# Gated scan in a hybrid encoder: narrow TensorE products regrouped, key scales moved to the first queries, last columns scaled wider apart

## The chip, the cores and the metric

The kernel runs on one core of a Trainium2 chip. Its time is device time in microseconds (us), the median of several runs. TensorE (PE) multiplies matrices, and its weight loads are shown apart (PEld). VectorE (DVE), ScalarE (ACT) and GpSimd (POOL) work elementwise; SyncE (SP) issues most transfers. Each engine takes its own instructions in their order and waits on semaphores for the others.

## The reference

One encoder layer on x of 1024 positions by 1024 channels, float32:

```
h  = RMSNorm(x);  P = h @ W_in
A  = conv module on its columns (GLU, depthwise conv of 31, LayerNorm, swish, pointwise)
B  = bidirectional gated scan, 8 heads of 128:  S_t = diag(f_t) S_{t-1} + k_t v_t^T,  o_t = S_t^T q_t
     f = lb + (1-lb) sigmoid(z),  k = (1-lb) sigmoid(-z), one scan forward and one backward
x  = x + W_out(sigmoid(gA) * A + sigmoid(gB) * B)
x  = x + W_down(silu(dwconv3(h2 W_gate)) * (h2 W_up)),  h2 = RMSNorm(x);  final RMSNorm
```

## The kernel before

Large products are done in three parts (high times high, high times low, low times high, `mm3`, lines 149 to 151), each a matmul of 128x512. They are the dense work, and the order on TensorE is the order in which the code is written, while the tile framework's scheduler orders the other engines.

The scan is worked off while dense products are still left. A head has 1024 positions, in two halves of 512, so there are 16 halves `i`. For each half two things run side by side:

- `scan_base` prepares keys `kG` (two directions) and queries `qF`: it doubles the span over which gates are multiplied in, 1, 2, 4, 8, 16, in place. Before each doubling ScalarE copies (`woven`, line 1176) the pairs of that level to pages `A` (8 of them in turn). Five steps, each ended by a `yield`. Step 3 issues the score products of the levels up to 4 (`level`, line 1195: 64 products of 32x32, 128 in the trace, where each float32 product shows twice).
- `scan_levels` goes on with the finished half: products of levels 8 and 16 into a bank `ob`, then zeros (`none`, line 1302) and blocks of 32 into a bank `sc`, doubling 32, blocks of 64 (line 1281), doubling 64. `scan_states` then transposes `kG` (line 1320, called kT here) and makes the states from it (line 1329, into `u`).

So a half has five places `n` = 0 to 4, and at the end of each `between` is called: it issues some dense products (`FILL` is 1.77 pieces, a piece is 6 matmuls, so 6 or 12), one step of the next half's preparation (`ahead`), and one step of the outputs of the head before (`pending`: 11 products of line 1370, at places 1 and 2 of even halves, or four transposes of line 1396, at places 1 and 2 of odd halves). The blocks, the levels up to 4 and the first `u` take the two banks `sc` in turn.

At the very end, `last_jobs` makes the last part of the down projection: 8 column jobs for positions 0 to 511, 8 for the next 256, 8 for the last 256 (`PARTS`). A job has 4 pieces. Each job's result is transposed some pieces later (`turn_out`, line 1890), squared on ScalarE (line 1892) and multiplied by the norm weight on VectorE (line 1905). When a part is done, `scale_out` scales each 128 positions by the row's norm, 640 columns on VectorE (line 1928) and 384 on ScalarE (line 1926), and stores them. `later(n, ...)` puts something off by n pieces.

Of the kernel before, what the change touches and what calls it, by code (L numbers as in the profile page):

```python
# [15 lines left out]
ALU = mybir.AluOpType  # L16
# [3 lines left out]
FILL = 1.77  # L20
# [7 lines left out]
GLU_FILL = 2  # L28
GLU_MORE = 4
GLU_LATE = 17  # L30
BASE_STEPS = 1
ALIGN = 128
H = 512
EPS = 1e-6
# [14 lines left out]
def tile_hybrid_encoder(  # L49
# [51 lines left out]
    def bank(tag):  # L101
        return ps.tile([P, H], F32, tag=tag, name=nm(tag), bufs=BANKS[tag])
# [56 lines left out]
    def later(n, do):  # L159

        chores.append([n, do])
# [981 lines left out]
    def tt(o, a, b, op=ALU.mult):  # L1143
        V.tensor_tensor(o, a, b, op=op)  # L1144
# [7 lines left out]
    def scan_inputs(i):  # L1152


        h, half = divmod(i, 2)
        q = page(hp, "q", 2)
        f = hp.tile([P, 2, H], F32, tag="f", name=nm("f"), bufs=2)
        kG = hp.tile([P, 2, H], F32, tag="kG", name=nm("kG"), bufs=3)
        nc.sync.dma_start(q, d_q[h][half])
        for d in range(2):  # L1160
            z = page(hp, "zi", 3)
            nc.sync.dma_start(z, d_z[d][h][half])
            A.activation(kG[:, d, :], z, AF.Sigmoid, scale=-1.0)
            A.activation(z, z, AF.Sigmoid)
            A.activation(f[:, d, :], z, AF.Identity, scale=oml_of(d, h), bias=lb_of(d, h))
        V.tensor_scalar(f, f, MIN_FORGET, 1.0, op0=ALU.max, op1=ALU.min)
        return q, f, kG, kscale[:, h : h + NH + 1 : NH]

    def pairs(t, h, other=H):

        return view(t, 0, [[other + h, 2], [2 * h, H // (2 * h)], [1, h]])
# [7 lines left out]
    def slot(b, n):  # L1179
        return b[:, n * P : (n + 1) * P]  # L1180
# [7 lines left out]
    def each():  # L1188
        for c in range(4):
            for g in range(0, P, 32):  # L1190
                yield c * P + g, slice(g, g + 32), slice(32 * c, 32 * c + 32)

    def level(b, A_t, Q_t):
        for at, g, o in each():
            T.matmul(b[g, o], A_t[:, at : at + 32], Q_t(at), start=True, stop=True)

    def row(t):
        return lambda at: t[:, at : at + 32]
# [18 lines left out]
    def scan_base(ins):  # L1217


        q, f, kG, ks = ins  # L1220
        qF = hp.tile([P, 2, H], F32, tag="qF", name=nm("qF"), bufs=4)
        D_t = hp.tile([P, 4, 32], F32, tag="D", name=nm("D"), bufs=3)
        for d in range(2):
            V.tensor_scalar(kG[:, d, :], kG[:, d, :], ks[:, d : d + 1], None, op0=ALU.mult)
        k_d, Q1 = page(hp, "A", 8), page(hp, "A", 8)
        tt(k_d, kG[:, 0, :], kG[:, 1, :], ALU.add)
        A1 = woven(kG, 1)
        odd = H // 2
        tt(
            pairs(Q1, 1, 0),  # L1230
            view(q, 0, [[1, 2], [2, odd], [1, 1]]),
            view(f, H, [[1 - H, 2], [2, odd], [1, 1]]),
        )
        tt(
            view(qF, 1, [[H - 1, 2], [2, odd]]),
            view(q, 1, [[-1, 2], [2, odd]]),
            view(f, H + 1, [[-(H + 1), 2], [2, odd]]),
        )
# [24 lines left out]
        A16, Q16 = woven(kG, 16), woven(qF, 16)  # L1263
        yield
        double_keys(kG, tb, 16)
        double_queries(qF, pairs(qF, 16), tb, 16)
        tb = totals(tb, 16)
        yield qF, kG, tb, D_t, A8, Q8, A16, Q16

    def scan_levels(base, S_t, Tt):  # L1270


        qF, kG, tb, D_t, A8, Q8, A16, Q16 = base

        def blocks(b, h):

            for c in range(0, H, P):
                for s0 in range(0, P, h):
                    t0 = s0 ^ h
                    d = s0 // h % 2  # L1280
                    T.matmul(  # L1281
                        b[s0 : s0 + h, c + t0 : c + t0 + h],
                        kG[:, d, c + s0 : c + s0 + h],
                        qF[:, 1 - d, c + t0 : c + t0 + h],
                        start=True,
                        stop=True,
                    )

        def double(tb, h, to=None):
            double_keys(kG, tb, h)  # L1290
            double_queries(qF, pairs(qF, h), tb, h)
            return totals(tb, h, to)

        b = bank("ob")
        level(slot(b, 0), A8, row(Q8))
        level(slot(b, 1), A16, row(Q16))
        for n, m in enumerate((m_8, m_16)):
            V.copy_predicated(D_t, over(m), near(slot(b, n)))
        yield
        b = bank("sc")  # L1300
        for at, g, _ in each():
            T.matmul(b[g, at : at + 32], none, none, start=True, stop=True)
        blocks(b, 32)
        tb = double(tb, 32)
        yield
        blocks(b, 64)
        double(tb, 64, view(Tt, 0, [[4, 2], [1, 4]]))
        A.copy(S_t, c4(b))
        for g in range(0, P, 32):
            nc.scalar.dma_start(S_t[g : g + 32, :, g : g + 32], D_t[g : g + 32])  # L1310
        yield
# [126 lines left out]

    NI = 2 * NH
    cur = Base(scan_inputs(0))  # L1440
    ins = scan_inputs(1)
    dense.fill(7)
    for pieces in (3, 4, 4, 3, 0):
        cur.step(1)
        dense.fill(pieces)
    pending = Stream(iter(()))
    for h in range(NH):
        Tt = hp.tile([P, 2, 2, 4], F32, tag="Tt", name=nm("Tt"), bufs=4)
        Sf = [hp.tile([P, 4, DK], F32, tag="st", name=nm("Sf"), bufs=4) for _ in range(2)]
        Sb = [hp.tile([P, 4, DK], F32, tag="st", name=nm("Sb"), bufs=4) for _ in range(2)]  # L1450
        kept = []
        for half in range(2):
            i = 2 * h + half
            base = cur.result()
            ahead = Base(ins) if i + 1 < NI else None
            ins = scan_inputs(i + 2) if i + 2 < NI else None

            def between(fill):
                dense.fill(fill)
                if ahead is not None:  # L1460
                    ahead.step(BASE_STEPS)
                pending.fill(1)

            S_t = hp.tile([P, 4, P], F32, tag="S", name=nm("S"), bufs=3)
            vl = load(d_v[h][half])
            for n, _ in enumerate(scan_levels(base, S_t, Tt[:, half])):
                if n == 1:
                    b = bank("tr")
                    for c in range(4):
                        T.transpose(b[:, c * P : (c + 1) * P], vl[:, c * P : (c + 1) * P], ident)  # L1470
                    v = hp.tile([P, 4, DK], F32, tag="v", name=nm("v"), bufs=3)
                    A.copy(v.rearrange("p c e -> p (c e)"), b)
                between(FILL)
            qF, kG = base[:2]
            for _ in scan_states(i, kG, v, Tt, Sf, Sb):
                between(FILL)
            kept.append((S_t, v, qF))
            cur = ahead
        pending = Stream(outputs(h, kept, Tt, Sf, Sb))

    dense.owed = 0
# [395 lines left out]
    def final_evac(i, half, chunks, acc):  # L1877
        t = xr[i][half][:, chunks[0] * P : (chunks[-1] + 1) * P]
        V.tensor_tensor(t, acc, t, op=ALU.add)
        later(4, lambda: turn_out(i, half, chunks))  # L1880

    def turn_out(i, half, chunks):

# [114 lines left out]
    fy = tc.alloc_tile_pool(name="fy", bufs=1, reuse_waits="tile")  # L1998
    st = Stream(run_jobs(last_jobs(LAST0, final_evac)))
    for n, part in enumerate(PARTS[:-1]):  # L2000
        st.fill(4 * ND * (n + 1) + 3 - st.count)
        finish(*part, late=2 + 2 * n)
    st.drain()
    advance_chores(1 << 10)
    finish(*PARTS[-1], late=0)
# [34 lines left out]
```

## Time and profile before

| | |
|---|---|
| median of 3 runs | 1736.81 us (1735.74 to 1737.69) |
| profiled execution | 1736.41 us, its span 1734.3 us |
| TensorE busy | 1709.2 us, 99% of the span; granted clock 0.998 |
| VectorE, ScalarE, GpSimd busy | 1255.9, 830.3, 170.4 us |
| scan, 505 to 860 us: TensorE, VectorE, ScalarE busy | 352.59, 286.16, 248.60 of 355 us |

TensorE is hardly ever idle, so a row of the timeline is best read by its start: the step from one start to the next is what an instruction costs in the stream (0.23 us for a dense matmul of 128x512, though its own row says 0.39).

### The profile page before, as it was taken

The page shows a single profiled execution, that of the slowest core. Times are in us where ns is not written, and L with a number is a line of the kernel's source. Part 1 is how long each engine was busy: PE and PEld are TensorE (multiplying, and loading weights), DVE is VectorE, ACT ScalarE, POOL GpSimd, SP SyncE. Part 2 cuts the span into 40 slices and gives each one's busy share as a digit, 9 for nine tenths or more (in the row PEclk, how much of TensorE's full clock was granted, in tenths as well). Part 3 has the DMA queues.
Part 4 walks back from the last instruction along what each step waited for, and adds up shares of the span by engine and source line. Part 5 has one row for each costly group of instructions (what it writes and reads, how often), then busy time and mean ns, then how long its engine had stood idle before and what let it go on. Part 6 is the DMA issues. An engine that isn't in the chain of part 4 may idle for free.

```text
span 1734.3 us, 30669 instructions
## 1 busy us (share of the span) xinstructions
PE 1709.2 (99%) x11902; PEld 1415.0 (82%) x11902; DVE 1255.9 (72%) x1937; ACT 830.3 (48%) x1544; POOL 170.4 (10%) x185
## 2 busy tenths in 40 slices
PE   8999999999999999999999999999999999999997
PEld 6878888888788888888878888888888888888787
DVE  5599999746778888888557466667767776657865
ACT  7444443334566777776442245444434433542334
POOL 2211111100000000000000002011111111000110
PEclk9999999999999999999999999999999999999999
DMA  8768888854673444435579466568777776783842
GB/s 288 239 167 184 193 194 193 197 167 154 207 230 104 131 126 132 127 115 192 175 248 333 147 207 205 146 148 170 158 170 160 180 172 153 229 267 107 205 91 98
DMA packets 343751, 308.27 MB, mean 178 GB/s; under 512 B 25262, under 2 KB 255798, under 8 KB 343606
## 3 DMA queue, kind: packets, MB, share of 16 engines
q1 hardware_dynamic: 289590, 267.51, 48.7%
q0 software_dynamic: 44800, 37.76, 15.2%
q10 hardware_dynamic: 9216, 1.05, 0.4%
q8 instruction: 93, 1.52, 0.4%
q14 instruction: 52, 0.43, 0.1%
HBM read 201.40 MB, written 87.03 MB: 166 GB/s over the span
## 4 chain that ended last, share of the span: by engine, by line
PE 44%; DMA 2%; DVE 2%; ACT 1%; issue 1%; SPq 0%; POOL 0%; POOLq 0%; ACTq 0%; DVEq 0%
PE mm L151 10%; PE mm L150 10%; PE mm L149 10%; PE sc L149 3%; PE sc L150 3%; PE sc L151 3%; PE tr L149 1%; PE tr L150 1%; PE tr L151 1%; DMA tm<-d_bm 1%; DVE hx L125 0%; DMA wr<-in_ffn_w_down_dram 0%; DMA wr<-wr 0%; DMA d_gc<-ft 0%; DVE wp L125 0%
## 5 line engine op out<-in xcount | busy, mean ns | idle before, releaser
L149 PE MATMUL mm<-hx,wp 128*128 128x512 f32 x1068 | 428.0, 401 | 3.3 <-ACT tm L851 2.1
L151 PE MATMUL mm<-hx,wp 128*128 128x512 f32 x1068 | 418.1, 391 | 0.9 <-DVE wp L125 0.8
L150 PE MATMUL mm<-hx,wp 128*128 128x512 f32 x1068 | 416.9, 390 | 0.3 <-DVE hx L125 0.2
L125 ACT CAST wp<-wr 128x1024 fp32r<-128x1024 f32 (+2 forms) x147 | 147.2, 1002 | 259.2 <-PE mm L150 119.5
L151 PEld LDWEIGHTS mm<-hx,wp 128*128 128x128 f32 x1068 | 200.9, 188 | 46.3 <-DVE wp L125 3.4
L149 PEld LDWEIGHTS mm<-hx,wp 128*128 128x128 f32 x1068 | 200.8, 188 | 46.1 <-ACT tm L851 2.6
L150 PEld LDWEIGHTS mm<-hx,wp 128*128 128x128 f32 x1068 | 201.2, 188 | 41.3 <-DVE hx L125 1.6
L125 DVE TENSOR_TENSOR wp<-wr,wp 128x1024 fp32r<-128x1024 f32 (+2 forms) x145 | 169.3, 1168 | 68.5 <-ACT wp L125 67.9
L1039 DVE SCALAR_TENSOR_TENSOR acc<-gl,v_b,acc 128x1024 f32<-128x1024 f32 x120 | 148.9, 1277 | 0.4
L1144 DVE TENSOR_TENSOR qF<-qF,tb 128x512 f32<-128x512 f32 x96 | 65.0, 684 | 20.8 <-ACT A L1176 20.7
L440 ACT COPY su<-mm 128x512 f32<-128x512 f32 x82 | 47.7, 582 | 66.2 <-PE mm L151 66.2
L149 PE MATMUL tr<-hx,wp 128*128 128x512 f32 x180 | 70.5, 392 | 0.0
L125 ACT CAST wq<-sw 128x1024 fp32r<-128x1024 f32 x41 | 43.2, 1053 | 56.3 <-PE mm L150 40.5
L151 PE MATMUL tr<-hx,wp 128*128 128x512 f32 x180 | 70.1, 389 | 0.0
L150 PE MATMUL tr<-hx,wp 128*128 128x512 f32 x180 | 70.0, 389 | 0.0
L1636 DVE SCALAR_TENSOR_TENSOR tm<-gp,v_a,tm 128x512 f32<-128x512 f32 x88 | 65.9, 749 | 3.9 <-ACT tm L1634 2.0
L1144 DVE TENSOR_TENSOR kG<-kG,tb 128x512 f32<-128x512 f32 x96 | 65.1, 684 | 3.7 <-PE sc L1281 3.7
L149 PE MATMUL mm<-hy,wp 128*128 128x512 f32 x164 | 64.2, 391 | 0.0
L149 PE MATMUL sc<-hy,wq 128*128 128x512 f32 x164 | 64.2, 391 | 0.0
L151 PE MATMUL sc<-hy,wq 128*128 128x512 f32 x164 | 63.8, 389 | 0.0
L150 PE MATMUL mm<-hy,wp 128*128 128x512 f32 x164 | 63.8, 389 | 0.0
L150 PE MATMUL sc<-hy,wq 128*128 128x512 f32 x164 | 63.8, 389 | 0.0
(372 smaller groups left out, 3609.9 us busy)
## 6 DMA issues: line engine op xcount, KB each, us to landing
wr<-in_w_in_dram SPq DMA_DIRECT2D x48, 512.0 KB
wr<-in_ffn_w_up_dram SPq DMA_DIRECT2D x22, 512.0 KB
sw<-in_w_in_dram SPq DMA_DIRECT2D x38, 256.0 KB
d_g<-ft SPq DMA_DIRECT2D x38, 256.0 KB
sw<-in_ffn_w_up_dram SPq DMA_DIRECT2D x38, 256.0 KB
sw<-in_ffn_w_up_dram POOLq DMA_DIRECT2D x19, 512.0 KB, 8.1
wr<-sw POOLq DMA_DIRECT2D x32, 256.0 KB, 3.8
wr<-wr POOLq DMA_DIRECT2D x32, 256.0 KB, 4.1
```

Source lines behind the costliest of these rows:

```text
L125: parts = A.copy(hi, src), eng.tensor_tensor(lo, src, hi.bitcast(F32), op=ALU.subtract)
L149: T.matmul(acc, whi[:, k, :], ahi, start=first, stop=False, skip_group_check=again)
L150: T.matmul(acc, whi[:, k, :], alo, start=False, stop=False, skip_group_check=again)
L151: T.matmul(acc, wlo[:, k, :], ahi, start=False, stop=last, skip_group_check=again)
L440: A.copy(t, acc)
L1039: V.scalar_tensor_tensor(acc, g[:, k : k + S], tap(k), acc, op0=ALU.mult, op1=ALU.add)
L1144: V.tensor_tensor(o, a, b, op=op)
L1636: V.scalar_tensor_tensor(c, g[:, o + k : o + k + H], vec("fdw", k * NF + j), c, op0=ALU.mult, op1=ALU.add,)
```

## The change

Three edits.

**Key scales.** Both directions of `kG` were multiplied by a scale in place, then added for `k_d`. Now `k_d` alone is made with the scales, `kG` stays unscaled, and the scale is a third factor in the four products that make the first queries (`gated`).

**Places.** The zeros and the blocks of 32 stand right behind levels 8 and 16 at place 0; their bank `S_b` is held until the blocks of 64, which stay at place 2. In `between` the outputs now come ahead of the preparation step, and the preparation runs one place sooner: step 1 of half i+2 at place 4 of half i, steps 2 to 5 of half i+1 at places 0 to 3 of half i.

**End.** Transposes of the two small parts come 6 pieces after their job (4 before); the rows are scaled 6 pieces apart (2 and 4 before), the second part's from 2 pieces later on.

```diff
-        for d in range(2):
-            V.tensor_scalar(kG[:, d, :], kG[:, d, :], ks[:, d : d + 1], None, op0=ALU.mult)
         k_d, Q1 = page(hp, "A", 8), page(hp, "A", 8)
-        tt(k_d, kG[:, 0, :], kG[:, 1, :], ALU.add)
+        V.tensor_scalar(k_d, kG[:, 1, :], ks[:, 1:2], None, op0=ALU.mult)
+        V.scalar_tensor_tensor(k_d, kG[:, 0, :], ks[:, 0:1], k_d, op0=ALU.mult, op1=ALU.add)
         A1 = woven(kG, 1)
         odd = H // 2
-        tt(
-            pairs(Q1, 1, 0),
-            view(q, 0, [[1, 2], [2, odd], [1, 1]]),
-            view(f, H, [[1 - H, 2], [2, odd], [1, 1]]),
-        )
...
+        def gated(to, at, t, d):
+            V.scalar_tensor_tensor(
+                view(to, at, [[2, odd]]),
+                view(q, t, [[2, odd]]),
+                ks[:, d : d + 1],
+                view(f, d * H + t, [[2, odd]]),
+                op0=ALU.mult,
+                op1=ALU.mult,
+            )
+
+        for t in range(2):
+            gated(Q1, t, t, 1 - t)
+        for t in (1, 0):
+            gated(qF, (1 - t) * H + t, t, t)
...
         level(slot(b, 1), A16, row(Q16))
+        S_b = bank("sc")
+        for at, g, _ in each():
+            T.matmul(S_b[g, at : at + 32], none, none, start=True, stop=True)
+        blocks(S_b, 32)
         for n, m in enumerate((m_8, m_16)):
             V.copy_predicated(D_t, over(m), near(slot(b, n)))
-        yield
-        b = bank("sc")
-        for at, g, _ in each():
-            T.matmul(b[g, at : at + 32], none, none, start=True, stop=True)
-        blocks(b, 32)
         tb = double(tb, 32)
         yield
+        yield
+        b = S_b
         blocks(b, 64)
...
+            following = Base(scan_inputs(i + 2)) if i + 2 < NI else None
+
+            def between(n):
+                dense.fill(FILL)
                 pending.fill(1)
+                step_of = ahead if n < 4 else following
+                if step_of is not None:
+                    step_of.step(1)
...
-        later(4, lambda: turn_out(i, half, chunks))
+        later(8 - len(chunks), lambda: turn_out(i, half, chunks))
...
-        st.fill(4 * ND * (n + 1) + 3 - st.count)
-        finish(*part, late=2 + 2 * n)
+        st.fill(4 * ND * (n + 1) + (3, 5)[n] - st.count)
+        finish(*part, late=6)
```

On TensorE the narrow products (32 or 64 columns wide) lie in visits between products of full width. In half 3, before, first levels 8 and 16 (bank `ob`), then the blocks of 32 and the transposes of `v` (line 1470); dense products and the 16 zeros are left out at the dots:

```order
L1195 MATMUL ob_5713<-A_5596,A_5594 32x32 x16
L1195 MATMUL ob_5713<-A_5658,A_5656 32x32 x16
L149 MATMUL mm_5641<-hx_1027,wp_5111 128x512
...
L151 MATMUL mm_5763<-hx_581,wp_5443 128x512
...
L1281 MATMUL sc_5789<-qF_5372,kG_4978 32x32 x16
L1470 MATMUL tr_5826<-ident,tm_5711 128x128 x4
```

The same place of the changed kernel:

```order
L1194 MATMUL ob_5733<-A_5572,A_5570 32x32 x16
L1194 MATMUL ob_5733<-A_5638,A_5636 32x32 x16
...
L1284 MATMUL sc_5766<-qF_5305,kG_4996 32x32 x16
L148 MATMUL mm_5657<-hx_1027,wp_5126 128x512
...
L1475 MATMUL tr_5843<-ident,tm_5731 128x128 x4
```

The blocks of 32 have moved ahead of twelve dense matmuls, into the visit of levels 8 and 16; the transposes of `v` stand alone.

Further on in the same half, TensorE again, before: the blocks of 64 after four output transposes, dense products, the levels up to 4 of the next half, and kT:

```order
L1396 MATMUL tr_5857<-ident,tm_5485 128x128 x4
L1281 MATMUL sc_5789<-qF_5372,kG_4978 64x64 x8
L149 MATMUL mm_5763<-hx_679,wp_5442 128x512
...
L1195 MATMUL sc_5887<-q_5307,A_5774 32x32 x16
L1195 MATMUL sc_5887<-A_5775,A_5777 32x32 x16
L1195 MATMUL sc_5887<-A_5847,A_5845 32x32 x16
L1195 MATMUL sc_5887<-A_5855,A_5853 32x32 x16
L1396 MATMUL tr_5960<-ident,tm_5610 128x128 x4
L1320 MATMUL tr_5968<-ident,kG_4978 128x128 x4
```

and now:

```order
L1400 MATMUL tr_5862<-ident,tm_5489 128x128 x4
L1194 MATMUL sc_5870<-q_5326,A_5701 32x32 x16
L1194 MATMUL sc_5870<-A_5702,A_5705 32x32 x16
L1194 MATMUL sc_5870<-A_5833,A_5831 32x32 x16
L1194 MATMUL sc_5870<-A_5841,A_5839 32x32 x16
L1284 MATMUL sc_5766<-qF_5305,kG_4996 64x64 x8
L148 MATMUL mm_5820<-hx_679,wp_5458 128x512
...
L1400 MATMUL tr_5965<-ident,tm_5614 128x128 x4
L1324 MATMUL tr_5985<-ident,kG_4996 128x128 x4
```

The levels have moved ahead, directly before the blocks of 64, and between the blocks of 64 and kT there are now only dense products and an output step. Over the whole scan the order of before has 64 narrow visits. That of the change has 33; 15 of them are a visit of levels that goes straight on into blocks of 64.

VectorE around doubling 64 of half 3 (its last axis has 64 elements; 16 is the doubling of the next half), before:

```order
L1398 SCALAR_TENSOR_TENSOR ev_5862<-tr_5857,v_a,og_5495 128x512
L1144 TENSOR_TENSOR kG_4978<-kG_4978,tb_5824 128x2x4x64
L1144 TENSOR_TENSOR qF_5372<-qF_5372,tb_5824 128x2x4x64
L1144 TENSOR_TENSOR kG_5309<-kG_5309,tb_5954 128x2x32x8
L1144 TENSOR_TENSOR tb_6198<-tb_6134 128x256
L1144 TENSOR_TENSOR qF_5770<-qF_5770,tb_5954 128x2x32x8
L1144 TENSOR_TENSOR kG_5309<-kG_5309,tb_6004 128x2x16x16
```

and now:

```order
L1402 SCALAR_TENSOR_TENSOR ev_5867<-tr_5862,v_a,og_5499 128x512
L1143 TENSOR_TENSOR tb_6060<-f_5716 128x512
L1143 TENSOR_TENSOR qF_5699<-qF_5699,tb_5937 128x2x32x8
L1143 TENSOR_TENSOR kG_5328<-kG_5328,tb_5979 128x2x16x16
L1143 TENSOR_TENSOR kG_4996<-kG_4996,tb_5803 128x2x4x64
L1143 TENSOR_TENSOR qF_5305<-qF_5305,tb_5803 128x2x4x64
```

The doubling 64 of `kG`, for which kT waits, stood ahead of doublings 8 and 16 of the next half; now it stands behind the query part of 8 and the key part of 16.

More of the change, by code (lines that the diff above doesn't have):

```diff
@@ L30 @@
 GLU_LATE = 17
-BASE_STEPS = 1
 ALIGN = 128
@@ L1222, in scan_base @@
         D_t = hp.tile([P, 4, 32], F32, tag="D", name=nm("D"), bufs=3)
-        for d in range(2):
-            V.tensor_scalar(kG[:, d, :], kG[:, d, :], ks[:, d : d + 1], None, op0=ALU.mult)
         k_d, Q1 = page(hp, "A", 8), page(hp, "A", 8)
-        tt(k_d, kG[:, 0, :], kG[:, 1, :], ALU.add)
+        V.tensor_scalar(k_d, kG[:, 1, :], ks[:, 1:2], None, op0=ALU.mult)
+        V.scalar_tensor_tensor(k_d, kG[:, 0, :], ks[:, 0:1], k_d, op0=ALU.mult, op1=ALU.add)
         A1 = woven(kG, 1)
         odd = H // 2
-        tt(
-            pairs(Q1, 1, 0),
-            view(q, 0, [[1, 2], [2, odd], [1, 1]]),
-            view(f, H, [[1 - H, 2], [2, odd], [1, 1]]),
-        )
[L1234 to L1238, printed above, removed]
+        def gated(to, at, t, d):
[11 more added lines that the diff above has]
+            gated(qF, (1 - t) * H + t, t, t)
         double_keys(kG, f, 1)
@@ L1440, in tile_hybrid_encoder @@
     cur = Base(scan_inputs(0))
-    ins = scan_inputs(1)
+    ahead = Base(scan_inputs(1))
     dense.fill(7)
@@ L1445, in tile_hybrid_encoder @@
         dense.fill(pieces)
+    ahead.step(1)
     pending = Stream(iter(()))
@@ L1454, in tile_hybrid_encoder @@
             base = cur.result()
[L1455 to L1461, printed above, removed]
+            following = Base(scan_inputs(i + 2)) if i + 2 < NI else None
+            def between(n):
+                dense.fill(FILL)
                 pending.fill(1)
+                step_of = ahead if n < 4 else following
+                if step_of is not None:
+                    step_of.step(1)
             S_t = hp.tile([P, 4, P], F32, tag="S", name=nm("S"), bufs=3)
@@ L1472, in tile_hybrid_encoder @@
                     A.copy(v.rearrange("p c e -> p (c e)"), b)
-                between(FILL)
+                between(n)
             qF, kG = base[:2]
-            for _ in scan_states(i, kG, v, Tt, Sf, Sb):
-                between(FILL)
+            for n, _ in enumerate(scan_states(i, kG, v, Tt, Sf, Sb)):
+                between(3 + n)
             kept.append((S_t, v, qF))
-            cur = ahead
+            cur, ahead = ahead, following
         pending = Stream(outputs(h, kept, Tt, Sf, Sb))
```

## The prediction

> **What bounds the kernel now.** First the page's share of each engine, then the windows over the scan:
>
> ```profile
> PE 1709.2 (99%) x11902; PEld 1415.0 (82%) x11902; DVE 1255.9 (72%) x1937; ACT 830.3 (48%) x1544; POOL 170.4 (10%) x185
> 505.00:860.00 355.00, 352.59 (x5718) 295.95 (x5707) 286.16 (x627) 248.60 (x558) 12.87 (x14) 1.00 0.43 135
> ```
>
> TensorE is the bound, at a full clock, in the scan as elsewhere: 352.59 of 355 us, while VectorE (286.16) and ScalarE (248.60) have room. So little is to be had from waits; what counts is what TensorE's stream costs. No matmul is added or removed by the change, only their order, so I looked in the timeline for what the order costs. Rows of TensorE, first the initial levels alone, then three visits to narrow products in half 0, and four transposes alone near the end:
>
> ```profile
> 504.03 0.39 PE L151 MATMUL mm<-hx,wp 128*128 128x512 f32 x1
> 504.35 0.46 PE L1195 MATMUL sc<-q,A 128*32 128x32 f32 x32
> 504.62 1.07 PE L1195 MATMUL sc<-A,A 128*32 128x32 f32 x96
> ...
> 506.20 0.39 PE L151 MATMUL mm<-hx,wp 128*128 128x512 f32 x1
> ...
> 515.05 0.39 PE L151 MATMUL mm<-hx,wp 128*128 128x512 f32 x1
> 515.37 0.76 PE L1195 MATMUL ob<-A,A 128*32 128x32 f32 x64
> 516.06 0.50 PE L149 MATMUL mm<-hx,wp 128*128 128x512 f32 x1
> 516.40 0.39 PE L150 MATMUL mm<-hx,wp 128*128 128x512 f32 x1
> 516.63 0.40 PE L151 MATMUL mm<-hx,wp 128*128 128x512 f32 x1
> ...
> 517.32 0.40 PE L151 MATMUL mm<-hx,wp 128*128 128x512 f32 x1
> 517.65 0.28 PE L1302 MATMUL sc<-none 128*32 128x32 bf16 x16
> 517.76 0.47 PE L1281 MATMUL sc<-qF,kG 128*32 128x32 f32 x32
> 518.16 0.66 PE L1470 MATMUL tr<-ident,tm 128*128 128x128 f32 x4
> ...
> 519.11 0.40 PE L151 MATMUL mm<-hx,wp 128*128 128x512 f32 x1
> ...
> 521.19 0.39 PE L151 MATMUL mm<-hx,wp 128*128 128x512 f32 x1
> 521.51 0.69 PE L1281 MATMUL sc<-qF,kG 128*64 128x64 f32 x16
> ...
> 522.69 0.40 PE L151 MATMUL mm<-hx,wp 128*128 128x512 f32 x1
> ...
> 883.02 0.39 PE L151 MATMUL mm<-hx,wp 128*128 128x512 f32 x1
> 883.26 0.60 PE L1396 MATMUL tr<-ident,tm 128*128 128x128 f32 x4
> ...
> 884.16 0.40 PE L151 MATMUL mm<-hx,wp 128*128 128x512 f32 x1
> ```
>
> Read the starts. A dense matmul takes one step of 0.23 us (516.40 to 516.63). From the last dense start ahead of a visit to the third behind it there are three such steps, 0.69 us, and the visit. So levels 8 and 16 (64 products) cost 516.63 - 515.05 - 0.69 = 0.89 us, the levels up to 4 (128 products) 506.20 - 504.03 - 0.69 = 1.48, the blocks of 64 cost 522.69 - 521.19 - 0.69 = 0.81, zeros, blocks of 32 and the transposes of v 519.11 - 517.32 - 0.69 = 1.10, and four transposes alone 884.16 - 883.02 - 0.69 = 0.45.
>
> Twice the products cost not twice as much: 64 more for 0.59 us, 0.0092 each. So of the 0.89 only 0.59 are products, and **0.30 us is the price of going in and out**: 0.09 on the way in (515.05 to 515.37 is 0.32, not 0.23), the rest on the way out. The zeros, 16 for 0.11, are followed by the blocks of 32 without such a step.
>
> **The change part by part.** *Blocks of 32 into the visit of levels 8 and 16.* Before, the two cost 0.89 + 1.10 = 1.99 us a half. Now there is one visit: 0.30 in and out, 0.59 for the levels, 0.11 for the zeros, 32 x 0.0092 = 0.29 for the blocks, and 0.45 for the transposes of v, which stand alone: 1.74. That is 0.25 us a half, and 16 halves give **-4.0 us**. All rows are there, so I give this no range.
>
> *Levels up to 4 and blocks of 64 in one visit*, 15 times. One way in and out goes, 0.30 us, but in the middle the width changes from 32 to 64, and no row shows that. Below, it costs nothing, as from zeros to blocks of 32; above, it costs the whole 0.30. The nearest row is the way from blocks of 32 into transposes, also a change of width without dense work between: 517.76 to 518.16 is 0.40 for products of 0.29, so 0.11. I take that: 0.19 each, **-2.9 us**, between 0 and -4.5.
>
> The Trainium skill (TensorEngine Tiling (Array Packing), Key Properties) says that a change of the tiling mode drains TensorE, and going to another tile in the same mode does not. The zeros and the blocks of 32 agree with it (no step), and by it the passage from 32 to 64 is not free; were it as dear as a whole visit's way in and out, this term would be 0 and the sum 2.9 us less.
>
> *Waits that go.* The waits over the scan (490 to 880 us), total, times, longest:
>
> ```profile
> PEld sc L1281 <- DVE qF L1144: 2.9, 4, 1.3
> PE sc L1281 <- DVE qF L1144: 2.0, 2, 1.0
> DVE qF L1144 <- ACT A L1176: 20.7, 13, 3.7
> ACT A L1176 <- DMA S<-D: 7.9, 3, 2.8
> ```
>
> The blocks of 64 wait for doubling 32 on VectorE, for they come one fill of dense work behind the blocks of 32. Now two fills (18 to 24 matmuls, 4.1 to 5.5 us), v and the levels lie between, against two operations of 0.68. This wait goes: **-2.5 us**, between 2.0 (TensorE's own idle time) and 2.9 (its weight loads').
>
> *Waits that come.* Mean times of the operations, by shape:
>
> ```profile
> L1144 DVE TENSOR_TENSOR qF<-qF,tb 128x512 f32<-128x512 f32 x96 | 65.0, 684 | 20.8 <-ACT A L1176 20.7
> L1337 DVE SCALAR_TENSOR_TENSOR Sf<-Sf,Tt,sc 128x128 f32<-128x128 f32 x48 | 16.5, 345 | 0.8
> L1224 DVE TENSOR_SCALAR kG<-kG,kscale 128x512 f32<-128x512 f32 x32 | 15.3, 481 | 17.6 <-ACT kG L1163 17.5
> L1398 DVE SCALAR_TENSOR_TENSOR ev<-tr,v_a,og 128x512 f32<-128x512 f32 x14 | 10.4, 744 | 0.5 <-PE tr L1396 0.5
> L1176 ACT COPY A<-kG 128x512 f32<-128x512 f32 x80 | 51.5, 644 | 14.0 <-DVE kG L1144 13.6
> L1176 ACT COPY A<-qF 128x512 f32<-128x512 f32 x64 | 40.6, 634 | 31.4 <-DVE qF L1144 10.4 <-PE sc L1195 9.9 <-DMA S<-D 7.9
> ```
>
> kT waits for doubling 64 of kG, which VectorE now has, in 12 of 16 halves, behind doubling 8 of the queries and 16 of the keys; and ScalarE can copy the queries of level 8 only when the levels up to 4 have freed their page. From the end of the levels: copy 0.63, doubling 8 0.68, doubling 16 0.68, doubling 64 0.68, together 2.67, or 3.15 where the key scale for k_d (0.48) stands between. TensorE meanwhile has the change of width 0.11, blocks of 64 0.51, the way out 0.21, 6 or 12 dense matmuls (1.38 or 2.76) and, in odd halves, four transposes (0.45): 2.66 or 4.04. Even halves from the third on have eleven output products there and more room. Only odd halves with 6 matmuls fall short, and by the order of the dense work these are two (halves 3 and 9), by 0 to 0.5 us and the hand-offs between engines, which no row above prices: 0.7 each, 1.4 us. The other place is the levels up to 4, which come a place sooner after levels 8 and 16 have freed the pages. In odd halves VectorE does doubling 32 and 2 (four times 0.68), the clamp and the masks, and ScalarE a copy, some 5 us; TensorE has 5.6 at least. I allow 0.3 us in three halves, 0.9. Together **+2.3 us**, between 0.5 and 6: the lower end if only the two halves fall short, the upper if half of the halves wait for 0.7 us.
>
> *The bank of S and earlier preparation.* Blocks of 32 and 64 now hold one sc bank from place 0 to 2 and the levels the other from place 1, while u, the third user, comes at place 4 as before; VectorE reads u in four operations of 0.345, 1.4 us, and the next user of that bank comes two fills later. Nothing. The inputs are loaded at the same place as before.
>
> *Third factor.* Off go two scalings (0.96), one sum and two products (0.68 each), 3.0 us a half. In come one scaling 0.48, one operation of two at 128x512 (0.744), and four at 128x256, for which 0.48 is taken between 0.345 at 128 and 0.744 at 512: 3.14. So VectorE has 0.1 us more a half, 2 us in all, within its 69 us of free time: **0**. If that cover were gone it would be +2.
>
> *The end.* The timeline where the first part's rows are scaled:
>
> ```profile
> 1701.44 0.28 PE L151 MATMUL mm<-hx,gx 128*128 128x256 f32 x1
> 1701.48 2.13 ACT L1926 ACTIVATE y<-y,frs 128x384 f32<-128x384 f32 x4 [0.47 <-POOL frs L1902]
> 1703.27 0.41 PE L1890 MATMUL sc<-ident,xr 128*128 128x128 f32 x2 [1.54 <-ACT y L1926]
> ```
>
> Four scalings in a row keep ScalarE from the squares of the last transposes, so their bank is not free and TensorE waits 1.54 us. In the changed order one scaling (2.13 / 4 = 0.53) stands between squares of two transposes, and the transposes come two pieces later. This wait goes: **-1.5 us**, between 1.0 and 1.6. The two last transposes stand behind the last dense product as before, so the tail behind it stays.
>
> **The sum.** -4.0 - 2.9 - 2.5 + 2.3 - 1.5 = -8.6 us against the profiled execution's 1736.41, so 1727.8. The median of the runs shown is 0.4 above that execution; with it the forecast is **1728.2 us**. The terms' ends together give -12.5 (no cost in the middle, few waits) and -1.0, which is 1724.3 to 1735.8.
>
> **The rivals.** *Slower: the wait of kT spreads.* The mechanism is the chain above, at the end of place 2. It holds no hand-offs and assumes that ScalarE copies at once. But ScalarE also squares outputs and issues the transfers of S; three times it stood 2.8 us at such a transfer, and VectorE stood 20.7 us in all at ScalarE's copies. If ScalarE came 1.2 us late in every half beyond the slack, that would be 16 x 1.2 = 19 us for the 1.4 counted: 1728.2 + 17.8 = 1746. From 0.63 us a half on, (8.6 + 1.4) / 16, the change is lost. For it speaks that VectorE's order puts doubling 64 behind what waits for ScalarE; against it that TensorE's waits in the scan were only some 3 us with as many such chains, and that most halves have over 0.8 us of room. Chance 0.10.
>
> *Faster by less: the middle step costs all, waits come back.* With 0.30 us for the change of width and waits of 4.5 us the sum is 8.6 - 2.9 - 2.2 = 3.5: 1733.3 us. For it speaks that VectorE works 286 of 355 us and in order. Chance 0.15, half of it within 3.5 us of no change.
>
> *More: no middle step, hardly a wait.* 8.6 + 1.6 + 1.8 = 12.0: 1724.8, and a little under it. Against it speaks the 0.11 of the nearest row. Chance 0.12.
>
> **How the numbers follow.** The forecast's own case has 0.63. About 0.2% (3.5 us) can be told from no change. Faster by more: 0.63 + 0.12 + 0.07 = 0.82. Within: the other 0.08. Slower: 0.10. The range takes in the less and the more, with a us or two at the lower end for what is unknown, and leaves out the slow rival: 1722.5 to 1735.5.
>
> **What would show it.** Right: in the changed timeline, levels 8 and 16 with blocks of 32 cost 1.29 us between dense rows, the levels and blocks of 64 about 2.1 together, and the waits no longer name line 1281's blocks of 64; at the end no 1.54. Wrong: TensorE's waits at kT (ACT or DVE kG) over 3 us, or the levels-and-blocks visit at 2.3 or more. The forecast as a whole is wrong if TensorE's idle time in the scan grows by over 5 us.

## The result, and the profile after

| | before | after |
|---|---|---|
| median | 1737.62 us (1735.23 to 1740.27, 12 runs) | 1734.28 us (1731.76 to 1736.78, 12 runs) |
| ratio | | 0.9981, 95% interval 0.9972 to 0.999 |
| profiled execution, its span | 1736.41, 1734.3 us | 1732.47, 1730.7 us |

The change is worth 3.3 us (1.7 to 4.9), where 8.6 were forecast. The median lies inside the forecast's range, near its slow end, but what moved it is not what the forecast added up. To find the place, both profiled executions were cut at four rows of the timeline: the first levels, the last output transposes of the scan, and the first and last transposes of the end.

| stretch | before | after | forecast |
|---|---|---|---|
| up to the first levels | 504.4 | 503.0 | 0 |
| scan, from the first levels to the last output transposes | 385.2 | 386.0 | -7.1 |
| between scan and end | 786.7 | 785.0 | 0 |
| end, from its first to its last transpose | 49.5 | 48.1 | -1.5 |
| rest | 8.6 | 8.6 | 0 |

The third stretch has the same code in both, the first but for the preparation of the first half; over all kernels of this document the third was anything from 785.0 to 791.9. So their -3.1 us can't be put down to the change. What the change touches is the scan, which did not get shorter at all, and the end, which in this pair fell by the forecast 1.5. The windows over the scan, before and after; the columns are length, then busy time of TensorE, its weight loads, VectorE, ScalarE and GpSimd, clock, DMA share, GB/s:

```profile
504.35:889.51 385.16, 382.75 (x5932) 321.72 (x5932) 299.35 (x652) 261.73 (x595) 14.70 (x16) 1.00 0.45 142
```

```profile
502.97:889.00 386.03, 378.48 (x5933) 323.27 (x5932) 302.50 (x669) 257.73 (x596) 14.69 (x16) 1.00 0.45 142
```

TensorE's busy time fell by 4.3 us and its idle time rose from 2.4 to 7.6 (length less busy), by just over the 5 us named as the point at which the forecast as a whole is wrong: the regrouping saved work, and waiting took it back. The timeline of TensorE in the first half of the kernel after shows the saving:

```profile
513.67 0.39 PE L150 MATMUL mm<-hx,wp 128*128 128x512 f32 x1
513.99 0.75 PE L1194 MATMUL ob<-A,A 128*32 128x32 f32 x63
...
514.69 0.52 PE L1284 MATMUL sc<-qF,kG 128*32 128x32 f32 x32
515.13 0.50 PE L148 MATMUL mm<-hx,wp 128*128 128x512 f32 x1
515.47 0.40 PE L149 MATMUL mm<-hx,wp 128*128 128x512 f32 x1
515.71 0.39 PE L150 MATMUL mm<-hx,wp 128*128 128x512 f32 x1
...
519.60 0.39 PE L150 MATMUL mm<-hx,wp 128*128 128x512 f32 x1
519.92 0.46 PE L1194 MATMUL sc<-q,A 128*32 128x32 f32 x32
520.19 1.07 PE L1194 MATMUL sc<-A,A 128*32 128x32 f32 x96
521.19 0.69 PE L1284 MATMUL sc<-qF,kG 128*64 128x64 f32 x16
521.81 0.50 PE L148 MATMUL mm<-hx,wp 128*128 128x512 f32 x1
522.14 0.39 PE L149 MATMUL mm<-hx,wp 128*128 128x512 f32 x1
522.37 0.40 PE L150 MATMUL mm<-hx,wp 128*128 128x512 f32 x1
```

Read by starts as before, levels 8 and 16 with blocks of 32 cost 515.71 - 513.67 - 0.69 = 1.35 us, and the levels up to 4 with blocks of 64 cost 522.37 - 519.60 - 0.69 = 2.08. The waits of TensorE in the scan (us in total, times, longest), after, show what was paid:

```profile
PE tr L1324 <- DVE kG L1143: 4.7, 3, 2.2
PE sc L1333 <- ACT kT L1326: 1.4, 2, 0.7
PE sc L1194 <- ACT A L1175: 1.3, 2, 1.0
```

The blocks of 64 are gone from this list. In their place stand the transposes into kT, waiting for doubling 64 of the keys (4.7 us, over the 3 that the prediction named as its sign of being wrong); u, waiting for the copy of kT; and the levels, waiting for a copy on ScalarE.

To put one number on each kind of visit, I took for every visit of the scan its cost over three dense steps, by starts as above, and subtracted the cheapest visit of its kind. What is over is waiting, whether the trace draws it as idle or as a long row (before, the levels share kT's visit in all but one of the odd halves, and what is over there is counted with the levels):

| us over the cheapest visits | before | after |
|---|---|---|
| kT (odd halves, after the output transposes) | 0 | 7.1 |
| u | 0.6 | 2.4 |
| blocks of 64, levels up to 4 | 2.6 and 1.1 | 2.0, now one visit |
| all visits of the scan | 5.3 | 13.1 |

(About 0.4 of the 13.1 is no wait: one visit of levels 8 and 16 reads 0.03 us cheaper than the fifteen others.)

The longest wait at kT, in the timeline of all engines, after, with rows of ScalarE, VectorE and TensorE; the first shows where VectorE was last idle, the rest is from the blocks of 64 on:

```profile
712.32 0.70 DVE L1165 TENSOR_SCALAR f<-f 128x1024 f32<-128x1024 f32 x1 [2.67 <-ACT f L1164]
...
717.03 1.05 ACT L124 CAST wp<-wr 128x1024 fp32r<-128x1024 f32 x1
717.19 0.69 PE L1284 MATMUL sc<-qF,kG 128*64 128x64 f32 x16
...
717.98 0.61 ACT L802 ACTIVATE ev<-mm 128x512 f32<-128x512 f32 x1
...
718.47 0.62 ACT L1175 COPY A<-qF 128x512 f32<-128x512 f32 x1
...
719.00 0.75 DVE L1402 SCALAR_TENSOR_TENSOR ev<-tr,v_a,og 128x512 f32<-128x512 f32 x1
...
719.66 1.22 DVE L124 TENSOR_TENSOR wp<-wr,wp 128x1024 fp32r<-128x1024 f32 x1
...
720.79 0.69 DVE L1143 TENSOR_TENSOR qF<-qF,tb 128x512 f32<-128x512 f32 x1
721.39 0.69 DVE L1143 TENSOR_TENSOR kG<-kG,tb 128x512 f32<-128x512 f32 x1
721.51 0.62 ACT L1175 COPY A<-qF 128x512 f32<-128x512 f32 x1 [1.25 <-DVE qF L1143]
721.58 1.90 ACTq L1314 DMA_DIRECT2D S<-D x3
...
722.14 1.11 PE L1324 MATMUL tr<-ident,kG 128*128 128x128 f32 x4 [2.24 <-DVE kG L1143]
```

The copy of the queries of 8 (718.47) comes behind a cast of dense weights (1.05) and an output copy (0.61) on ScalarE. Doubling 8 of the queries (720.79) and doubling 64 of the keys (721.39) come behind an output product (0.75) and the split of those weights (1.22) on VectorE. None of these four is part of the chain from the levels to kT, and all are ahead in order. But the copy ended at 719.09, and VectorE was not free for doubling 8 before 720.79, so in VectorE's order ScalarE's late copy held up nothing in this half: the last thing waited for was VectorE's own queue. The windows of VectorE's unbroken runs before the two longest waits, half 3 and half 9, say the same (the fourth number is VectorE's busy time):

```profile
578.04:587.95 9.91, 8.24 (x178) 6.69 (x176) 9.91 (x17) 7.76 (x15) 0.00 (x0) 1.00 0.51 163
712.32:722.08 9.76, 7.58 (x175) 6.20 (x173) 9.72 (x17) 7.89 (x16) 0.00 (x0) 0.99 0.41 134
```

In all five halves that wait at kT, VectorE has no idle time of over 0.1 us from 3.3 to 5.7 us ahead of the blocks of 64 until doubling 64 is done. What it waited for on ScalarE came ahead of that, and in four of the five it was the gates `f` of a later half (2.67 us in the first row above), not the copy of the queries.

The last row of ScalarE's queue (ACTq) is another cost that the busy times don't hold: issuing transfers into S.

### The profile page after: what moved, and what is told of

It reads as the page before. It is cut to its first block, busy times and chain, and to the rows that moved or that the text cites. A ratio compares the mean times of both kernels' runs of the same rounds, so it can differ in the third digit from the quotient of the medians.

```text
span 1730.7 us, 30713 instructions
## 1 busy us (share of the span) xinstructions
PE 1702.4 (98%) x11902; PEld 1415.8 (82%) x11902; DVE 1257.2 (73%) x1953; ACT 824.4 (48%) x1544; POOL 170.6 (10%) x185
## 3 DMA queue, kind: packets, MB, share of 16 engines
q10 hardware_dynamic: 9216, 1.05, 0.4%
```

## The experiments

Three theories for the waits. Theory 1: doubling 64 of the keys is queued on VectorE behind operations that hang on ScalarE. Theory 2: ScalarE itself is late, from issuing the transfers into S. Theory 3: the third factor takes VectorE's room.

All ratios are to the kernel before, run beside it on the same chip. The kernels ran in groups on different chips, so ratios are to be compared and not medians (5 to 12 runs each). Scan and waits are from one profiled execution each; two pairs with nearly the same scan code differ by 0.1 us (after, old key scales) and 0.6 (before, end alone). "kT" is the kT row of the table above.

| kernel | median us | ratio (95%) | scan | TensorE idle in it | kT | u |
|---|---|---|---|---|---|---|
| before, after | 1737.62, 1734.28 | 0.9981 (0.9972 to 0.999) | 385.2, 386.0 | 2.4, 7.6 | 0, 7.1 | 0.6, 2.4 |
| old key scales | 1735.12 | 0.9987 (0.9972 to 1.0001) | 386.1 | 8.2 | 6.9 | 2.2 |
| end alone | 1737.57 | 0.9998 (0.9988 to 1.0008) | 385.7 | 3.1 | 0 | 1.3 |
| doubling 64 first | 1731.62 | 0.9965 (0.9952 to 0.9979) | 381.6 | 5.5 | 3.6 | 1.6 |
| transfers on GpSimd | 1734.17 | 0.9973 (0.9963 to 0.9982) | 381.4 | 5.6 | 5.2 | 0.1 |
| blocks of 32 alone | 1734.98 | 0.9985 (0.9972 to 0.9998) | 383.7 | 3.7 | 0 | 1.2 |
| preparation alone | 1738.24 | 1.0006 (0.9994 to 1.0018) | 389.8 | 8.1 | 6.7 | 3.1 |
| both edits | 1728.37 | 0.9955 (0.9941 to 0.9969) | 377.3 | 2.3 | 2.4 | 0.0 |
| both edits, fixed dealing | 1727.91 | 0.995 (0.9937 to 0.9962) | 376.9 | 1.7 | 1.0 | 0.7 |
| fixed dealing alone | 1732.36 | 0.9973 (0.9963 to 0.9983) | 383.4 | 6.4 | 2.7 | 3.9 |
| before, transfers on GpSimd | 1739.46 | 1.0004 (0.9993 to 1.0016) | 383.5 | 2.6 | 0 | 0.0 |
| blocks of 32 alone, transfers on GpSimd | 1731.36 | 0.9963 (0.9951 to 0.9975) | 377.9 | 0.3 | 0 | 0.6 |

**Old key scales.** The kernel after, with the key scaling of before.

```diff
-        V.tensor_scalar(k_d, kG[:, 1, :], ks[:, 1:2], None, op0=ALU.mult)
...
+        for d in range(2):
+            V.tensor_scalar(kG[:, d, :], kG[:, d, :], ks[:, d : d + 1], None, op0=ALU.mult)
...
```

> The changed kernel with the old scaling of the keys: two scalings in place, a sum, and two products without the third factor; places and end as in the change. Theory 1 and 2: within 1.5 us of the change, kT's waits still 4 us or more. Theory 3: the waits at kT, u and the levels fall by half (from 11.4 to under 6 us), and the time by 4 us or more.

Scan 386.1 and kT 6.9, against 386.0 and 7.1: the third factor neither costs nor saves in the scan, and theory 3 falls. VectorE is full just ahead of the waits, but not by the third factor.

**End alone.** The kernel before with the edits of the end.

```diff
-        later(4, lambda: turn_out(i, half, chunks))
+        later(8 - len(chunks), lambda: turn_out(i, half, chunks))
...
-        finish(*part, late=2 + 2 * n)
+        finish(*part, late=6)
```

> The kernel before with the third edit alone (transposes and scaling of the last columns wider apart). All theories, and the prediction: 1.5 us less than before, all of it between the first and the last transpose of the end (49.5 us before, 48.0 then); the scan stays at 385.2 us within 1.

In the profile the end took 48.4 us against 49.5, so -1.1; the times (0.9998, 0.9988 to 1.0008) hold up to 2.1 us of gain and can't tell 1.1 from nothing.

**Doubling 64 first.** The kernel after, with doubling 64 of the keys ahead of doubling 8 of the queries and 16 of the keys on VectorE: `issue_after` keeps these two behind the last doubling 64 in the order.

```diff
...
+    def behind(here):
+        return tc.issue_after(last64[0]) if here and last64 else contextlib.nullcontext()
...
-        tt(pairs(kG, h), pairs(kG, h), view(tb, 1, [[nb - 1, 2], [2, n], [0, h]]))
+        with behind(h == 16):
+            i = tt(pairs(kG, h), pairs(kG, h), view(tb, 1, [[nb - 1, 2], [2, n], [0, h]]))
+        if h == 64:
+            last64[:] = [i.ins]
...
-        tt(pairs(qF, h), q, view(tb, nb + 1, [[-(nb + 1), 2], [2, n], [0, h]]))
+        with behind(h == 8):
+            tt(pairs(qF, h), q, view(tb, nb + 1, [[-(nb + 1), 2], [2, n], [0, h]]))
```

> The changed kernel, but the key part of doubling 64 is issued on VectorE ahead of the query part of doubling 8 and the key part of doubling 16 of the next half. Theory 1 (kT waits because doubling 64 is queued behind operations that wait for ScalarE): in the changed kernel the visits of four transposes and kT in odd halves cost 7.1 us more than seven times the cheapest of them (1.32 us); that falls to 0 to 2 us, the scan (386.0 us from the first levels to the last output transpose) to about 380.5, the whole to 5 us below the change. Theory 2 (ScalarE is late because it issues the transfers of S, 0.64 us each): the waits only move to the next places, u and the levels, whose 2.4 and 1.9 us grow by as much as kT's fall, and the time stays within 1.5 us of the change. Theory 3 (VectorE has too much to do with the third factor): the same as theory 2.

The scan is 4.4 us shorter than after, kT half of what it was; 0 to 2 us were expected by theory 1, and 3.6 are left. The wait that stays longest, in this kernel's timeline:

```profile
718.52 0.74 DVE L1412 SCALAR_TENSOR_TENSOR ev<-tr,v_a,og 128x512 f32<-128x512 f32 x1
...
719.18 1.21 DVE L125 TENSOR_TENSOR wp<-wr,wp 128x1024 fp32r<-128x1024 f32 x1
...
720.51 0.68 DVE L1144 TENSOR_TENSOR kG<-kG,tb 128x512 f32<-128x512 f32 x1
...
721.24 0.66 PE L1334 MATMUL tr<-ident,kG 128*128 128x128 f32 x4 [1.84 <-DVE kG L1144]
```

The scan's own operations no longer stand ahead of doubling 64 there; the output product and the weights' split still do, 1.95 us together, about the 1.84 that TensorE waits. No kernel here moves these two, so that they are the cause of what is left is argued and not shown.

**Transfers on GpSimd.** The kernel after, one word changed.

```diff
-            nc.scalar.dma_start(S_t[g : g + 32, :, g : g + 32], D_t[g : g + 32])
+            nc.gpsimd.dma_start(S_t[g : g + 32, :, g : g + 32], D_t[g : g + 32])
```

> The changed kernel, but the four transfers of D into S of each half are issued by GpSimd, which is idle in the scan, not by ScalarE. Theory 1: kT's 7.1 us stay at 4 or more, since in the rows of the longest wait ScalarE came late by a cast and an output copy, not by a transfer; the time falls by under 2 us. Theory 2: kT, u and the levels wait under 4 us together (11.4 now), and the time falls by 5 us or more.

The issues in the kernel after: shortest, median and longest ns, and from when to when.

```profile
L1314 ACTq DMA_DIRECT2D S<-D x64: 592/612/1323, 523.1 to 856.5; - x64
```

Added up, the 64 issues take 41 us of the scan's 386, 0.64 each on the mean. That isn't in ScalarE's 257.73 us of busy time. Without it the scan is 4.6 us shorter, u's waits are gone (2.4 to 0.1) and kT falls from 7.1 to 5.2. Theory 2 had kT, u and the levels under 4 together, so that is a part of it. The Trainium skill (DMA: Bandwidth & Descriptors, "Issuing engines are not separate DMA queues") says that starting transfers on several engines saves only the sequencer's time to start them, which is usually small beside the transfer. It is smaller here too, with 0.61 against 2.5 us from issue to landing in the median, but it is that time which counts: 2.6 us a half on an engine whose copies are in the chain.

Theories 1 and 2 thus each hold in part: the order on VectorE and the issuing on ScalarE each cost some 4.5 us of scan. (Of theory 1 it is the order that is shown; that what stands ahead of doubling 64 waits for ScalarE there is not what the rows of the longest wait say.) The times alone don't show it of one edit: both intervals (0.9952 to 0.9979, 0.9963 to 0.9982) overlap that of the kernel after. The next four kernels ask which part of the change brings the waits, and whether the two remedies add.

**Blocks of 32 alone.** The kernel after with the next half's preparation at the places of before, and ahead of the outputs again.

```diff
-    ahead.step(1)
...
+            ahead = Base(ins) if i + 1 < NI else None
+            ins = scan_inputs(i + 2) if i + 2 < NI else None
...
+                if ahead is not None:
+                    ahead.step(BASE_STEPS)
                 pending.fill(1)
-                step_of = ahead if n < 4 else following
...
```

> The kernel after with one part undone: the preparation of the next half at the places that it had before (started at the half's own first visit); blocks of 32 stay behind levels 8 and 16. Theory A (the waits at kT come with the preparation a place sooner, which puts the levels' copies and the queries of 8 between the doublings of 32 and 64): the visits of levels 8 and 16 with blocks of 32 keep their 1.35 us, waits at kT stay under 1.5 us in all as in the kernel before, the wait of blocks of 64 for doubling 32 goes; scan 380 to 382 us against 385.2 before, ratio to before about 0.998, so about as fast as the kernel after or a little faster. Theory B (the waits come with blocks of 32 a place sooner, whatever the preparation does): waits at kT of 5 us and more, scan 386 to 388, ratio about 1.001.

**Preparation alone.** The kernel after with blocks of 32 back in the visit of the transposes of v.

```diff
         level(slot(b, 1), A16, row(Q16))
-        S_b = bank("sc")
-        for at, g, _ in each():
-            T.matmul(S_b[g, at : at + 32], none, none, start=True, stop=True)
-        blocks(S_b, 32)
...
+        yield
+        b = bank("sc")
+        for at, g, _ in each():
+            T.matmul(b[g, at : at + 32], none, none, start=True, stop=True)
+        blocks(b, 32)
...
-        yield
-        b = S_b
...
```

> The kernel after with the other part undone: blocks of 32 in the visit behind levels 8 and 16's as before (with the transposes of v), the preparation a place sooner as after. Theory A: the levels up to 4 and blocks of 64 share a visit (2.1 us), but the waits at kT are 5 to 8 us and blocks of 64 wait as before for doubling 32 (2 us): scan 386 to 388 us, ratio to before 1.000 to 1.001. Theory B: waits at kT under 2 us, scan 381 to 383, ratio 0.998.

Their waits of TensorE in the scan, blocks of 32 alone first:

```profile
PE ob L1375 <- DVE Sb L1427: 2.7, 3, 1.4
PE sc L1334 <- ACT kT L1327: 0.9, 1, 0.9
```

```profile
PE tr L1323 <- DVE kG L1143: 4.6, 4, 2.0
PE sc L1332 <- ACT kT L1325: 2.0, 3, 1.2
PE sc L1284 <- DVE qF L1143: 1.2, 1, 1.2
```

Theory A holds for the waits: those at kT come with the preparation a place sooner (6.7 us there, 0 without it), and that edit by itself makes the scan 4.6 us longer, to 389.8 where 386 to 388 were expected; its ratio is 1.0006, no gain. Blocks of 32 alone make the scan 1.5 us shorter, less than the 3 to 5 expected, because of a wait that no theory had: the output products wait for the backward states `Sb`, 2.7 us. So of the change's two parts in the scan only one was a gain.

**Both edits.** Doubling 64 first, and the transfers on GpSimd (the two diffs above together).

> The kernel after with two edits together: the key part of doubling 64 queued on VectorE ahead of the query part of doubling 8 and the key part of doubling 16, and the transfers of the mask's blocks into S issued by GpSimd in place of ScalarE. If the two causes are separate (theories 1 and 2 each hold in part), their gains add: waits over the cheapest visits about 4 us in all (13.1 after, 9.4 and 7.1 with one edit each), kT 1 to 3 us, scan 377 to 379.5 us, ratio to before 0.995. If both edits remove the same wait, scan is 381 as with either alone and the ratio 0.9965.

**Both edits, fixed dealing.** The same, with dense steps dealt out by place, so that two pieces always lie ahead of kT.

```diff
+FILLS = (2, 1, 2, 2, 1.85)
...
-                dense.fill(FILL)
+                dense.fill(FILLS[n])
```

> The same two edits, and the dense steps dealt out in fixed numbers by place (2, 1, 2, 2 and 1.85 in place of 1.77 at each), so that two steps always stand between blocks of 64 and the transposes into kT. If the rest of the wait at kT is a place with one dense step where the chain needs two: waits at kT under 0.5 us, scan 376.5 to 378, ratio to before 0.994. If the one step fewer ahead of blocks of 64 makes the levels or blocks of 64 wait instead, their visits carry 2 us or more over their cheapest and scan is 379 to 382.

**Fixed dealing alone.** The kernel after with this last diff only.

> The kernel after with nothing changed but the dealing of dense steps (2, 1, 2, 2 and 1.85 by place in place of 1.77 at each). If the waits at kT stood in the halves in which one dense step alone lies between blocks of 64 and kT: they fall from 7.1 us to 2 to 3, scan 381 to 383, ratio to before 0.9965 (0.9981 for the kernel after). If they come from the order on VectorE and from ScalarE's time whatever the dealing: kT keeps 5 us or more, or the levels and u take over what it loses, scan 385 to 387, ratio 0.998 to 0.999.

The two remedies add in the scan, 4.4 + 4.6 us singly and 8.7 together, as expected of separate causes. Fixed dealing then takes kT from 2.4 to 1.0, where under 0.5 was expected, and the times (0.9955 and 0.995) can't tell the two apart. Alone it takes kT from 7.1 to 2.7, but u rises from 2.4 to 3.9, and the scan is 383.4, just over the 381 to 383 expected: a part of the wait moved on to the next place. The two versions with both edits are the fastest measured, with intervals that lie wholly below 1 and below that of the kernel after.

**Before, transfers on GpSimd**, and **blocks of 32 alone, transfers on GpSimd**: the one-word diff on the kernel before, and on blocks of 32 alone.

> The kernel before with the transfers of the mask's blocks into S issued by GpSimd in place of ScalarE, nothing else. Theory A (ScalarE's time for issuing them was covered by slack in the kernel before, and the preparation a place sooner takes that slack): waits of blocks of 64 and u fall by no more than 1 to 1.5 us, scan 383.5 to 385, ratio to before 0.999 to 1.000. Theory B (the issuing cost the same in both kernels): scan falls by 4 to 5 us as it did in the kernel after, to 380.5, ratio 0.997.

> The kernel after with the preparation at the places that it had before (blocks of 32 behind levels 8 and 16 kept), and the transfers into S issued by GpSimd. It tells whether the preparation a place sooner is worth having once its waits are gone. If it is worth its 3 us of visits: this kernel has scan at 381 to 383 us (383.7 with the transfers on ScalarE, 377.3 for the kernel after with both edits), ratio to before 0.998. If the shared visit of levels and blocks of 64 brought nothing by itself: scan 377 to 379, ratio 0.9955.

The waits of TensorE over the scan in the second, all that are listed:

```profile
PE mm L151 <- DVE wp L125: 0.3, 1, 0.3
PE ob L1375 <- DVE Sb L1427: 0.2, 1, 0.2
PE mm L149 <- DVE ev L1106: 0.2, 1, 0.2
```

The same word is worth 1.7 us of scan in the kernel before (and nothing that its time shows; the wait of blocks of 64 does not fall there, 2.6 and 3.2), but 4.6 after and 5.8 with blocks of 32 alone. So theory A of the first holds in the main, a little above its bound: by the lengths of the scan, ScalarE's time for issuing was mostly covered before and is not with blocks of 32 a place sooner, also where the preparation is not sooner. There the wait for `Sb` goes with it, from 2.7 to 0.2 us. Through which step the issuing held up `Sb` was not followed.

With that time gone, blocks of 32 alone have a scan of 377.9 us: within 0.6 of the 377.3 of both edits. The shared visit of levels and blocks of 64, the aim of the sooner preparation, then nets next to nothing: both edits together still wait 2.4 us at kT. Without doubling 64 first it is a loss: of the two kernels that differ only in the places of the preparation and the outputs, both with the transfers on GpSimd, the one with the sooner preparation has the longer scan, 381.4 against 377.9.

## Why the prediction failed, step by step

**Blocks of 32 into the visit of levels 8 and 16: right, a little large.** -4.0 was forecast; the two kinds of visits sum to 31.7 us before and 28.7 after, -3.0. The visit is 1.35 where 1.29 was worked out.

**Levels up to 4 with blocks of 64: right in the visit.** It costs 2.08, forecast about 2.1. By the prediction's own prices (0.30 in and out, 128 x 0.0092 for the levels, 0.51 for the blocks) the change of width from 32 to 64 costs 0.09, against 0.11 taken from the nearest row. The Trainium skill (TensorEngine Tiling (Array Packing), Key Properties) says that a change of mode drains TensorE; the 0.09 agrees with that, at a price far under a visit's 0.30. Between the cheapest visits of before and after lie 3.3 us for -2.9 forecast. But some of that was a wait in the rows of before: between the kernels with the transfers on GpSimd (blocks of 32 alone, both edits) the same merge is worth 0.13 to 0.19 a half, 2.4 in all.

**The wait of blocks of 64 goes: right.** 2.6 us over the cheapest before, and no such wait listed after; -2.5 was forecast.

**Waits that come: the step that failed.** +2.3 was forecast, 6 at most. Over the cheapest visits, kT brought 7.1 (1.4 forecast), u 1.8 (nothing), and the levels, whose visit now has 2.0 with the blocks of 64, 1.0 more than before (0.9): 9.9 us. With the rest of the visits' waits (-0.1) the scan's sum is -3.0 - 3.3 - 2.6 + 9.9 - 0.1 = +0.9, which is what the windows show. The place was right: kT waits behind doubling 64, and the two halves named, 3 and 9, the only odd ones with 6 dense matmuls there, hold 1.9 and 3.7 of the 7.1 us. The size was wrong, 0.7 being allowed for each on no row's evidence; and three more of the seven odd halves behind output transposes wait, by 0.2, 0.4 and 0.9 us.

The step that failed is the sum of the chain, 2.67 us for a copy and the doublings 8, 16 and 64, as if the engines had nothing else to do between these links. In the longest case VectorE did seven operations on end from the blocks of 64 on, of which two were in the sum; an output product and a weights' split alone are 1.97 us. Doubling 64 was done at 722.08, 4.9 us after the blocks of 64 began. That VectorE had room (286 of 355 us) was true of the average and not of these stretches, where it was hardly ever idle. The prediction also looked for lateness at ScalarE's copies. VectorE's waits for these and for the gates over the scan (500 to 895 us), before:

```profile
DVE qF L1144 <- ACT A L1176: 20.7, 13, 3.7
```

and after:

```profile
DVE f L1165 <- ACT f L1164: 16.8, 7, 5.5
DVE qF L1143 <- ACT A L1175: 6.7, 11, 2.3
```

The waits for the copies fell from 20.7 to 6.7 us; 16.8 now stand at the gates, where it was 5.1 before (and 13.3 at the keys).

**ScalarE's issuing: overlooked as a term.** The rival with a late ScalarE named the transfers of S, but as a risk of 0.10, without the 0.64 us that each issue takes. What it read as waits for these transfers (7.9 us in three waits, so 2.6 each and 2.8 at most) is as long as four issues; in the kernel after such waits of ScalarE sum to 36 us. It needed 0.63 us a half to lose the whole forecast; the waits that came are 9.9 / 16 = 0.62 a half on the scan, so that rival's point was all but reached in the scan. In kind it came nearest to what happened there; its 19 us were not reached.

**Less, by another sum.** The rival "faster by less" has 3.5 us, and 3.3 were measured. That is luck: it took 0.30 for the change of width, which costs 0.09, and 4.5 for the waits, which are 9.9, and in the profiled pair scan and end together gave 0.6.

**Third factor 0: right**, by the kernel with the old scales. **End -1.5: right in kind, a little large.** The wait of 1.54 is gone, and 0.7 for `oj` stands in its place:

```profile
PE sc L1895 <- ACT oj L1897: 0.7, 1, 0.7
```

The stretch is 1.5 us shorter in the pair, 1.1 in the edit alone. Over all kernels here it took 48.1 to 50.0, mean 48.9, in the eleven profiles with the edit, and 49.5 and 50.5 in the two without: about -1.1.

**What stays open.** Scan and end together fell by 0.6 us in the profiled pair, the times by 3.3 (1.7 to 4.9). The other kernels with the sooner preparation and the transfers on ScalarE lean the same way: the old scales have +1.3 in scan and end by the profile and -2.3 by the ratio, preparation alone +3.9 and +1.0. It may be that kT waits less in executions other than the profiled ones; no run here tells it from chance in the rest of the program, which differs by up to 7 us between profiled executions. Nor does any kernel here take the output product or the weights' split out of VectorE's queue ahead of doubling 64, which would test the reading of the longest wait.

## What to carry to other kernels

Where a step is moved closer to its consumer, add up the chain from everything that its engines do between its links in their order, other work's operations and DMA issues included; a chain of the step's own operations is only a lower bound. Undo the parts of a regrouping one by one: here one part was worth 5.6 us of scan once ScalarE was free of issuing (383.5 to 377.9), and the other cost 4.6 when made alone. An engine's busy share over a stage is no measure of its room: it leaves out the issuing of transfers, and it hides stretches like the 9.9 us of half 3 in which VectorE, at 78% over the scan, was never idle.

## What the runs showed of the hardware

Issuing one small transfer held ScalarE's queue for 0.612 us in the median (592 ns at least, 64 times), beside copies of 0.62 us, with none of it in the busy time. GpSimd needed 0.552 for the same transfers, and they are counted as busy there (51.26 us of the scan against 14.69):

```profile
L1314 POOL DMA_DIRECT2D S<-D x64: 549/552/732, 524.3 to 852.8; - x64
```

Stretches of the same code differ more between executions than the effects sought: 785.0 to 791.9 us for the part between scan and end in 13 profiled executions, one of each kernel, whose mean clocks over the whole program are 0.995 to 0.999.
